# A hybrid decoder layer on one core: the two token halves of the blocked gate/up product become even and odd tiles, and TensorE's order between attention and gate/up is written down

## Chip, core and metric

The kernel runs on one core of a Trainium2 chip. The metric is the device time of one execution in microseconds (us); less is better. Engines are named as in the profile: PE is TensorE, DVE VectorE, ACT ScalarE, POOL GpSimd, SP SyncE, which here only issues DMAs.

## What is computed

One decoder layer on 1024 tokens of width 1024, in f32: an entry LayerNorm, two groups of attention heads, an output projection over the two normalised groups, a LayerNorm, a SwiGLU feed-forward of width 2816, and a last LayerNorm.

```python
h = layer_norm(x, ln_in_g, ln_in_b)
mix = hybrid_mixer(h, ...)                    # merged = [rms_norm(sb_out), rms_norm(swa_out)]; merged @ w_out
h = layer_norm(ALPHA * h + mix, ln1_g, ln1_b) # the stretch that the change rewrites ends here
gate, up = split(h @ w_gate_up)
ffn = (silu(gate) * up) @ w_down
h = layer_norm(ALPHA * h + ffn, ln2_g, ln2_b)
```

## The kernel before

Every f32 matrix product is done as three products of rounded parts (high x high, low x high, high x low), so each operand is first split: ACT casts the high part, and POOL or DVE subtracts it to get the low part. The tokens are eight tiles of 128.

The kernel has three large stretches. Up to about 490 us it projects and attends; the output projection of one head group runs beside the attention and leaves partial sums in `acc_dram`. From about 490 to 580 us comes the stretch of this change. From there to about 1085 us PE multiplies gate and up, and then the down projection follows.

In the stretch of the change `out_load` loads a pair of token tiles of the other head group (`m`), splits it and sums its squares. `out_proj` then goes through the two tiles: a 128x1 product `pr` gives the sum of squares, DVE and POOL make the RMS scale `r` of it, 24 products fill two PSUM tiles `pc` (12 for each half of the width), and DVE (L510) adds `pc` times `r` to the row sums `res`. `ln_apply` normalises `res` in place: DVE statistics (L121, L123, L114, L138), POOL's power for `rstd` (L115), ACT subtracts the mean (L141), DVE scales (L142), POOL adds the bias (L144). The last tile has a form without ACT (L131, L134). `h1_dram` keeps the result for the last LayerNorm.

Gate/up is done as a blocked product with seven instead of eight block products, P1 to P7 (`RIGHT` names their right-hand operands). The tokens are cut into two halves, and the width into `d0` and `d1`. The first half gives `B11` and `B21`, the second `B22`, and the differences of the halves give `T1` to `T4`. `put_b` fills them: four 128x128 transposes on PE into one of the two PSUM banks with the tag "tr", a cast by ACT, a subtraction by DVE. I call this a group. There are 28 of them: 2 for each of four tiles of the first half, 5 for each of the second.

Before the change the halves are tiles 0 to 3 and 4 to 7, so a tile of the second half needs the tile four places before. The pairs run in the order 0, 2, 1, 3 (L620), and each tile's groups are written right after its LayerNorm. The program says nothing of PE's order: Tile's scheduler sets it. Only SP's DMAs can be tied to the order in which they are written, by `Ordered`, and that is off here. All tiles of this stretch come from one pool of 17 buffers of 4 KB (`U`), of which 10 are held by the weights and the LayerNorm's gain and bias.

`prepare` splits the weights of the next blocks, which `left_of` sums by DVE first for P3 and P5 to P7; `gate_up` runs one block of 12 products of 512 columns and adds it up. `seq` is their order.

Of the kernel before, what the change touches and what calls it, by code (L numbers as in the profile page):

```python
# [21 lines left out]
P = 128  # L22
# [52 lines left out]
def layer(ctx: ExitStack, tc: tile.TileContext, x, ln_in, w_sw, w_sb, norm_g,  # L75
          sinks, rel_bias, onehot, w_out, ln1, w_gu, w_down, ln2, out):
    nc = tc.nc
    pe, act, dve, pool = nc.tensor, nc.scalar, nc.vector, nc.gpsimd
    sp = Ordered(tc, nc.sync)
# [142 lines left out]
    def U(shape, name, dt=F32R):  # L222
        return ub.tile(shape, dt, tag="u", name=name)
# [270 lines left out]

    def out_proj(c, m, wo, acc):
        mh, ml, ss = m
        for i in range(2):
# [121 lines left out]

    order = (0, 2, 1, 3)  # L620
    ms = {c: out_load(0, c) for c in order[:2]}
    hs = {}
    d0, d1 = slice(0, 512), slice(512, D)
    for n, c in enumerate(order):
        if n in (1, 2):
            ms[order[n + 1]] = out_load(0, order[n + 1])
        for t, h in out_proj(c, ms[c], wo, load_acc(c, acc_dram)):
            ln_apply(h, h, g1, b1, t == NT - 1)
            sp.dma_start(h1_dram[t], h)
            o = (t % 4) * P  # L630
            if t < 4:
                hs[t] = h
                put_b("B11", h[:, d0], o)
                put_b("B21", h[:, d1], o)
                continue
            h0 = hs.pop(t - 4)
            tt = U([P, 2, 512], "tt", F32)
            pool.tensor_tensor(out=h0[:, d0], in0=h[:, d0], in1=h0[:, d0], op=ALU.subtract)
            pool.tensor_tensor(out=tt[:, 0], in0=h[:, d1], in1=h0[:, d0], op=ALU.subtract)
            dve.tensor_tensor(out=tt[:, 1], in0=h[:, d1], in1=h[:, d0], op=ALU.subtract)  # L640
            pool.tensor_tensor(out=h0[:, d1], in0=h0[:, d1], in1=tt[:, 0], op=ALU.subtract)
            put_b("B22", h[:, d1], o)
            put_b("T2", tt[:, 0], o)
            put_b("T3", tt[:, 1], o)
            put_b("T1", h0[:, d0], o)
            put_b("T4", h0[:, d1], o)


# [3 lines left out]
    fs = [f for i in range(KF) for f in (i, KF + i)]  # L652

    seq = [(fs[0], "P1"), (fs[1], "P1"), (fs[0], "P2"), (fs[1], "P2"), (fs[0], "P6"), (fs[0], "P7")]
    seq += [(fs[0], n) for n in ("P5", "P4", "P3")] + [(fs[1], n) for n in ("P6", "P7", "P5", "P4", "P3")]
    for f in fs[2:]:
# [48 lines left out]

    banks, tmps, acts = {}, {}, {}

    def spill(k, a, b):
# [9 lines left out]
        act.dma_start(a_dram[k][:, 5:7], s[1])  # L718

    def gate_up(i):  # L720
        f, name = seq[i]
# [5 lines left out]
        if name == "P1":  # L727
            tmps[f] = new("t", [P, 2, 512], bufs=2)
            act.copy(tmps[f][:, 0], ps)
            return  # L730
        u2, u3 = tmps[f][:, 0], tmps[f][:, 1]
        if name == "P2":
            acts[f] = new("act", [P, 2, 512], bufs=4)
        a = acts.get(f)
        add = lambda out, x: dve.tensor_tensor(out=out, in0=x, in1=ps, op=ALU.add)  # L735
        if name == "P2":
            act.activation(a[:, 0], ps, AF.Silu)
        elif name == "P6":
            add(u2, u2)
# [15 lines left out]

    prepare(6)
# [4 lines left out]
    for i in range(len(seq)):  # L761
        prepare(i + 6)
        gate_up(i)
# [78 lines left out]
    with tc.tile_pool(name="dn", bufs=4, reuse_waits="tile") as dn:  # L842
        bq += [dn.tile([P, D], F32, tag="bq", bufs=KF + 2, name="bq") for k in range(KF)]
        h = [dn.tile([P, D], F32, tag="h", bufs=NT, name="h") for t in range(NT)]
        LEFT = {"P2": 1, "P4": 2, "P5": 3, "P6": 4, "P7": 5, "P3": 6}
        NEEDS = {"P5": (1,), "P2": (2,), "P3": (3,), "P6": (), "P7": (), "P4": ()}
# [4 lines left out]
        def one(t):  # L851
            ot = dn.tile([P, D], F32, tag="ot", bufs=2, name="ot")
            rows = slice(t * P, (t + 1) * P)
            if t < NT - 1:
# [13 lines left out]
        for name in ("P5", "P2", "P3", "P6", "P7", "P4"):  # L868
# [5 lines left out]
            for k in range(KF):  # L874
# [87 lines left out]
```

## Time and profile before

| | us |
|---|---|
| median of three runs | 1236.27 (1234.16 to 1238.58) |
| the profiled execution | 1236.33 |
| its span | 1234.6 |
| PE busy | 1151.2 (93%) |
| DVE / POOL / ACT busy | 867.5 / 750.0 / 570.9 |

Over the span PE is busy 93% of the time. The page's row of granted clock has its lowest places at the start, near 490 us, and between 530 and 580 us. So the stretch of this change is one of the few in which PE is neither always busy nor always at its full clock. The table gives totals; what the change is worth is read from that stretch alone, by the engines' rows there.

### The profile page before, as it was taken

The numbers are of one execution on the slowest core, as the hardware profiler recorded it, in microseconds if no ns is written. First come the engines' busy times: TensorE is split into PE (matmuls) and PEld (weight loads), VectorE is DVE, ScalarE is ACT, GpSimd is POOL, SyncE is SP. The second block draws the span as 40 slices with busy tenths as digits, with TensorE's granted clock in tenths as the row PEclk, the third lists the DMA queues.
The fourth block names the chain that finished last, engine by engine and source line by source line (L and its number), as shares of the span: only waits on it lengthen the run. The fifth ranks groups of instructions, "written<-read, shape, count | busy, mean of one in ns | idle before, by whom it ended". The sixth has DMA issues, their size and how long they took to land. (4 is left out here: it accounts for less than half of the span.)

```text
span 1234.6 us, 17707 instructions
## 1 busy us (share of the span) xinstructions
PE 1151.2 (93%) x6246; PEld 990.9 (80%) x6246; DVE 867.5 (70%) x1257; ACT 570.9 (46%) x1224; POOL 750.0 (61%) x682
## 2 busy tenths in 40 slices
PE   5698999999998998977999999999999999979997
PEld 4688999899997886765888888888888888757785
DVE  7885786787889894777765645656456349998645
ACT  4565677767678564233433222332232234425531
POOL 5514344556647877567877656666557455774694
PEclk9798999999999898987999999999999999989998
DMA  7213102020105525134333323333323269643441
GB/s 274 93 55 94 35 23 77 23 66 22 49 18 172 186 99 192 73 121 145 119 128 111 103 76 112 111 111 102 95 94 111 95 218 396 212 137 93 114 134 68
DMA packets 60054, 140.69 MB, mean 114 GB/s; under 512 B 7060, under 2 KB 18877, under 8 KB 59966
## 3 DMA queue, kind: packets, MB, share of 16 engines
q1 hardware_dynamic: 45406, 110.71, 28.1%
q10 hardware_dynamic: 14560, 28.85, 6.1%
q8 instruction: 49, 0.80, 0.3%
q14 instruction: 39, 0.32, 0.1%
HBM read 95.75 MB, written 41.17 MB: 111 GB/s over the span
## 5 line engine op out<-in xcount | busy, mean ns | idle before, releaser
L107 POOL TENSOR_TENSOR w<-s,w 128x512 fp32r<-128x512 f32 x88 | 124.1, 1413 | 119.2 <-ACT w L106 119.2
L154 PE MATMUL pp<-xh,whi 128*128 128x256 f32 x544 | 158.8, 293 | 0.0
L154 PE MATMUL pp<-xh,wlo 128*128 128x256 f32 x544 | 158.2, 291 | 0.0
L154 PE MATMUL pp<-xl,whi 128*128 128x256 f32 x544 | 157.5, 290 | 0.0
L776 PE MATMUL pd<-bhl,ahl 128*128 128x512 f32 x612 | 146.6, 400 | 10.0 <-DVE bhl L768 9.6
L776 PEld LDWEIGHTS pd<-bhl,ahl 128*128 128x128 f32 x612 | 117.0, 193 | 39.4 <-DVE bhl L768 14.9
L106 ACT CAST w<-s 128x512 fp32r<-128x512 f32 x88 | 54.4, 622 | 202.7 <-PE pgu L703 118.9
L768 POOL TENSOR_TENSOR ahl<-ar,ahl 128x512 fp32r<-128x512 f32 x63 | 92.6, 1477 | 59.1 <-ACT ahl L767 57.0
L735 DVE TENSOR_TENSOR t<-t,pgu 128x512 f32<-128x512 f32 x88 | 60.1, 683 | 96.6 <-PE pgu L703 96.2
L433 POOL TENSOR_TENSOR s<-s,s 128x127 f32<-128x127 f32 (+2 forms) x96 | 92.6, 969 | 37.7 <-DVE s L429 33.3
L154 PEld LDWEIGHTS pp<-xh,wlo 128*128 128x128 f32 x544 | 106.6, 196 | 1.2
L154 PEld LDWEIGHTS pp<-xl,whi 128*128 128x128 f32 x544 | 106.6, 196 | 1.0
L154 PEld LDWEIGHTS pp<-xh,whi 128*128 128x128 f32 x544 | 106.5, 196 | 0.6
L429 DVE TENSOR_TENSOR_SCAN s<-s,brk 128x128 f32<-128x128 f32 (+1 forms) x64 | 74.7, 1174 | 11.2 <-ACT s L420 10.6
L374 POOL TENSOR_TENSOR L<-L,rd 128x512 f32<-128x512 f32 (+1 forms) x32 | 30.9, 989 | 81.5 <-DVE rd L372 63.9
L110 ACT CAST at<-tra 128x256 fp32r<-128x256 f32 (+1 forms) x160 | 55.5, 356 | 52.7 <-DVE at L111 30.9
L768 DVE TENSOR_TENSOR bhl<-bq,bhl 128x512 fp32r<-128x512 f32 x51 | 67.8, 1338 | 8.2 <-ACT bhl L767 7.9
L111 DVE TENSOR_TENSOR at<-tra,at 128x256 fp32r<-128x256 f32 (+1 forms) x160 | 58.5, 383 | 15.8 <-ACT at L110 14.6
L107 POOL TENSOR_TENSOR w<-gr,w 128x512 fp32r<-128x512 f32 x44 | 61.2, 1405 | 2.3 <-ACT w L106 2.3
L703 PE MATMUL pgu<-B11h,w 128*128 128x512 f32 x176 | 59.1, 398 | 1.4 <-ACT w L106 1.4
L767 ACT CAST ahl<-ar 128x512 fp32r<-128x512 f32 x63 | 38.9, 619 | 43.0 <-POOL ahl L768 17.1
L703 PE MATMUL pgu<-T4h,w 128*128 128x512 f32 x176 | 57.9, 390 | 0.0
(222 smaller groups left out, 3351.2 us busy)
## 6 DMA issues: line engine op xcount, KB each, us to landing
ar<-a_dram SPq DMA_DIRECT2D x73, 256.0 KB, 2.9
a_dram<-act ACTq DMA_DIRECT2D x33, 512.0 KB, 2.6
gr<-in_w_gu SPq DMA_DIRECT2D x24, 512.0 KB, 3.6
ur<-in_w_gu SPq DMA_DIRECT2D x23, 512.0 KB, 3.5
bq<-in_w_down SPq DMA_DIRECT2D x44, 256.0 KB, 4.3
raw<-in_w_sb SPq DMA_DIRECT2D x12, 512.0 KB, 3.4
h_dram<-x ACTq DMA_DIRECT2D x8, 512.0 KB, 3.3
m<-o_dram SPq DMA_DIRECT2D x32, 128.0 KB, 3.0
```

The source lines that it names most:

```text
L106: act.copy(hi, raw)
L107: pool.tensor_tensor(out=lo, in0=raw, in1=_f(hi), op=ALU.subtract)
L110: act.copy(hi, ps)
L111: dve.tensor_tensor(out=lo, in0=ps, in1=_f(hi), op=ALU.subtract)
L154: pe.matmul(ps, a, b, start=(i == 0), stop=(i == n - 1))
L429: dve.tensor_tensor_scan(s2[:, 0:w][:, ::-1], s2[:, 0:w][:, ::-1], brk[:, 512 - w:][:, ::-1] if last else zero.broadcast_to([P, w]), 1.0 i ...
L433: pool.tensor_tensor(out=s1[:, 0:m], in0=s1[:, 0:m], in1=s2[:, 1:m + 1], op=ALU.mult)
L703: pe.matmul(ps, a, b, start=(start and n == 0), stop=(stop and n == 11), skip_group_check=True)
L735: add = lambda out, x: dve.tensor_tensor(out=out, in0=x, in1=ps, op=ALU.add)
L767: act.copy(w[:, 0], src)
L768: eng.tensor_tensor(out=w[:, 1], in0=src, in1=_f(w[:, 0]), op=ALU.subtract)
L776: pe.matmul(pd[t], x, y, start=(first and k == 0 and n == 0), stop=(end and k == KF - 1 and n == 2), skip_group_check=True)
```

## The change

1. The halves become even and odd tiles: `even(t)` fills B11 and B21 from tile t, `odd(t)` forms the differences of tiles t-1 and t and fills B22, T1, T3, T2, T4. Two of the differences are now written in place into the odd tile (except for the last one), which needs no further buffer.
2. The pairs run in the order 0, 1, 2, 3, and the groups of a tile are written two tiles behind: after tile t's products come `even(t-2)`, or B22 of `odd(t-2)`; the four T groups of an odd tile wait one tile more. They stand beside the next even tile's, so there are six groups in a row.
3. PE is wrapped in `Ordered` too, and from the first output projection to the last transposes PE's and SP's instructions keep the order in which they are written. The `pc` products go to the PSUM banks with the tags "z" and "av" instead of "pp".
4. The stores to `h1_dram` are issued by ACT instead of SP.
5. P1 and P2 of the first two features (48 products) are written before the last odd tile's transposes; their P1 results go into one tile `ut`, and their Silu comes later. The weights of nine blocks are prepared from the first load, where before those of the first feature were loaded and summed a second time.
6. The last LayerNorm finds its tiles by `tile_of`, since the halves now hold other tokens.

```diff
-    pe, act, dve, pool = nc.tensor, nc.scalar, nc.vector, nc.gpsimd
+    pe, act, dve, pool = Ordered(tc, nc.tensor), nc.scalar, nc.vector, nc.gpsimd
...
-                ps = bps.tile([P, 512], F32, tag="pp", name="pc")
+                ps = bps.tile([P, 512], F32, tag=banks[d], name="pc")
...
+    seq = [(f, n) for n in ("P1", "P2") for f in fs[:2]]
+    EARLY_GU = len(seq)
+    for f in fs[:2]:
+        seq += [(f, n) for n in ("P6", "P7", "P5", "P4", "P3")]
...
+    def even(t):
+        put_b("B11", hs[t][:, d0], t // 2 * P)
+        put_b("B21", hs[t][:, d1], t // 2 * P)
+
+    def odd(t):
+
+        x, y = hs[t - 1], hs[t]
+        o = t // 2 * P
+        sub(pool, x[:, d0], y[:, d0], x[:, d0])
+        if t < NT - 1:
+            t2, t3 = y[:, d1], y[:, d0]
...
+        sub(dve, t3, y[:, d1], y[:, d0])
+        put_b("B22", y[:, d1], o)
+        if t < NT - 1:
+            sub(pool, t2, y[:, d1], x[:, d0])
+        sub(pool, x[:, d1], x[:, d1], t2)
+        return lambda: [put_b(n, v, o) for n, v in (("T1", x[:, d0]), ("T3", t3), ("T2", t2), ("T4", x[:, d1]))]
...
+    pe.on = sp.on = True
+    for c in range(4):
+        if c in (1, 2):
+            ms.append(out_load(0, c + 1))
+        for t, h in out_proj(c, ms[c], wo, load_acc(c, acc_dram), ("z", "av")):
+            hs[t] = h
+            ln_apply(h, h, g1, b1, t == NT - 1)
+            act.dma_start(h1_dram[t], h)
+            if t >= 2 and t % 2 == 0:
+                even(t - 2)
+                if late:
+                    late.pop()()
+            elif t > 2:
+                late.append(odd(t - 2))
+    even(NT - 2)
+    late.pop()()
+    prepare(5)
+    for i in range(EARLY_GU):
+        gate_up(i)
+    prepare(EARLY_GU + 5)
+    odd(NT - 1)()
+    pe.on = sp.on = False
...
+        tile_of = [2 * (t % 4) + t // 4 for t in range(NT)]
...
-                        sp.dma_start(h[t], h1_dram[t])
+                        sp.dma_start(h[t], h1_dram[tile_of[t]])
```

On every engine the built programs are alike up to the end of the attention and again from about the eighth block of gate/up on; the difference lies between. Three places show it.

PE, behind the products of the first tile that has T groups to follow it. `pc` is a projection's PSUM tile, `pr` the 128x1 product that opens the next tile, `trh` the PSUM tile of a group (x4 is one group), `tt` and `res` what is transposed. Before:

```order
L154 MATMUL pc<-woh,wlo 128x512
L612 MATMUL trh<-ident,tt 128x128 x8
L612 MATMUL trh<-ident,res 128x128 x12
L612 MATMUL trh<-ident,tt 128x128 x8
L501 MATMUL pr<-ones,m 128x1
L154 MATMUL pc<-woh,whi 128x512
```

Now, behind tile 4:

```order
L65 MATMUL pc<-woh,wlo 128x512
L68 MATMUL trh<-ident,res 128x128 x24
L65 MATMUL pr<-ones,m 128x1
L65 MATMUL pc<-woh,whi 128x512
```

Seven groups stood in a row there, of the two tiles that had just been normalised; now it is six, of tiles 1 and 2, and so again behind tile 6 (six) and tile 7 (seven), with single tiles' worth of products between.

SP, at the loads of the third and fourth pair. `m` is an operand of the projection, `res` a tile's row sums, `gr` a gate weight. Before:

```order
L71 DMA res_6437<-acc_dram4_102 128x1024
L71 DMA res_6439<-acc_dram5_103 128x1024
L71 DMA h1_dram0_106<-res_6291 128x1024
L71 DMA h1_dram1_107<-res_6293 128x1024
L71 DMA h1_dram4_110<-res_6437 128x1024
L71 DMA h1_dram5_111<-res_6439 128x1024
L71 DMA m_6627<-o_dram0_90 128x256
```

Now:

```order
L71 DMA res_6411<-acc_dram3_101 128x1024
L71 DMA m_6540<-o_dram0_90 128x256
L71 DMA m_6540<-o_dram1_91 128x256
L71 DMA m_6540<-o_dram2_92 128x256
L71 DMA m_6540<-o_dram3_93 128x256
L71 DMA res_6552<-acc_dram4_102 128x1024
L71 DMA res_6554<-acc_dram5_103 128x1024
L71 DMA res_6713<-acc_dram6_104 128x1024
L71 DMA res_6715<-acc_dram7_105 128x1024
L71 DMA gr_6913<-in_w_gu 128x1024
```

The four stores, which wait for LayerNorms, no longer stand ahead of the loads; all loads up to the first gate weights follow each other.

DVE, behind the last tile's products, in the new program. `res_6715` is that tile's row sums, `s` the sums of weights of the first feature, `B22l`, `B11l` and `B21l` the low parts of groups:

```order
L510 SCALAR_TENSOR_TENSOR res_6715<-pc_6818,r_6816,res_6715 128x512
L652 TENSOR_TENSOR s_6931<-ur_6929 128x512
L654 TENSOR_TENSOR s_6932<-gr_6913,ur_6929 128x512
L121 BN_STATS bst_6846<-res_6715 128x6
L653 TENSOR_TENSOR s_6931<-s_6931,gr_6913 128x512
L510 SCALAR_TENSOR_TENSOR res_6715<-pc_6832,r_6816,res_6715 128x512
L655 TENSOR_TENSOR s_6932<-gr_6913,s_6931 128x512
L617 TENSOR_TENSOR B22l_6257<-trh_6860,B22h_6256 128x4x128
L121 BN_STATS bst_6846<-res_6715 128x6
L617 TENSOR_TENSOR B11l_6253<-trh_6869,B11h_6252 128x4x128
L123 BN_AGGR mv_6849<-bst_6846 128x2
```

The four sums of weights, which stood behind nearly all of the last groups before, now stand between the last tile's residual and the subtractions that free the transposes' banks.

## Rows read from the trace of the kernel before

**Rows 1.** Stretches: from:to, length, busy of PE, PEld, DVE, ACT, POOL; granted clock; DMA.

```profile
490.00:526.00 36.00, 34.14 (x157) 28.06 (x157) 23.27 (x49) 9.72 (x15) 21.49 (x23) 0.94 0.16 62
526.00:542.10 16.10, 8.84 (x38) 6.72 (x37) 9.62 (x18) 6.56 (x11) 11.89 (x10) 0.68 0.59 197
542.10:561.00 18.90, 18.10 (x93) 14.84 (x91) 15.78 (x31) 6.90 (x13) 10.23 (x11) 1.00 0.14 56
561.00:580.00 19.00, 11.09 (x45) 8.61 (x46) 15.28 (x21) 7.31 (x14) 14.84 (x12) 0.64 0.40 139
580.00:660.00 80.00, 80.00 (x355) 65.92 (x354) 51.43 (x57) 30.30 (x53) 59.50 (x42) 1.00 0.35 118
```

**Rows 2.** Timeline of PE: start, duration, instruction, [idle before it, and what ended it].

```profile
490.00 0.42 PE L501 MATMUL pr<-ones,m 128*128 128x1 f32 x2
...
513.21 0.39 PE L154 MATMUL pc<-woh,wlo 128*128 128x512 f32 x1
...
517.29 0.39 PE L154 MATMUL pc<-woh,wlo 128*128 128x512 f32 x1
...
525.79 1.04 PE L612 MATMUL trh<-ident,tt 128*128 128x128 f32 x8
527.85 0.66 PE L612 MATMUL trh<-ident,res 128*128 128x128 f32 x4 [1.02 <-DVE T2l L617]
531.04 1.31 PE L612 MATMUL trh<-ident,res 128*128 128x128 f32 x8 [2.53 <-DVE T3l L617]
533.54 1.94 PE L612 MATMUL trh<-ident,tt 128*128 128x128 f32 x8 [1.20 <-DVE T4l L617]
537.92 0.59 PE L501 MATMUL pr<-ones,m 128*128 128x1 f32 x2 [2.43 <-DVE res L510]
...
541.73 0.61 PE L154 MATMUL pc<-wol,whi 128*128 128x512 f32 x1
542.16 0.42 PE L154 MATMUL pc<-woh,wlo 128*128 128x512 f32 x1
...
561.50 0.66 PE L612 MATMUL trh<-ident,res 128*128 128x128 f32 x4 [0.79 <-POOL res L144]
...
575.69 0.79 PE L703 MATMUL pgu<-B11h,w 128*128 128x512 f32 x1 [1.43 <-ACT w L106]
...
581.36 0.60 PE L612 MATMUL trh<-ident,res 128*128 128x128 f32 x4
```

**Rows 3.** Timeline of SP's DMA queue: start of waiting, time to the last issue.

```profile
505.12 23.75 SPq L71 DMA_DIRECT2D h_dram<-res  x4
529.37 1.81 SPq L71 DMA_DIRECT2D m<-o_dram  x4
```

**Rows 4.** Timeline of DVE in the same stretch.

```profile
509.66 1.41 DVE L142 SCALAR_TENSOR_TENSOR res<-res,rstd,g 128x512 f32<-128x512 f32 x2
...
530.22 0.68 DVE L617 TENSOR_TENSOR T3l<-trh,T3h 128x512 fp32r<-128x512 f32 x1
530.82 0.67 DVE L617 TENSOR_TENSOR T1l<-trh,T1h 128x512 fp32r<-128x512 f32 x1
...
537.12 1.41 DVE L510 SCALAR_TENSOR_TENSOR res<-pc,r,res 128x512 f32<-128x512 f32 x2 [2.96 <-DMA res<-acc_dram]
...
540.29 0.68 DVE L121 BATCH_NORM_STATS2 bst<-res 128x6 f32<-128x512 f32 x1
541.01 0.21 DVE L123 BATCH_NORM_AGGREGATE mv<-bst 128x2 f32<-128x12 f32 x1
...
564.64 2.13 DVE L131 SCALAR_TENSOR_TENSOR res<-res,mv,g 128x1024 f32<-128x1024 f32 x1
```

**Rows 5.** Groups by line, whole span: busy, mean ns of one, idle before.

```profile
L681 DVE TENSOR_TENSOR s<-gr,ur 128x512 f32<-128x512 f32 x23 | 26.6, 1157 | 1.2 <-POOL w L107 1.2
```

**Rows 6.** Timelines of ACT and POOL: a group's cast, and two LayerNorm steps.

```profile
505.51 0.59 ACT L616 CAST B11h<-trh 128x512 fp32r<-128x512 f32 x1 [3.71 <-PE trh L612]
...
522.88 1.34 ACT L141 ACTIVATE res<-res,nmu 128x512 f32<-128x512 f32 x2 [2.05 <-DVE nmu L138]
...
525.59 2.94 POOL L144 TENSOR_TENSOR res<-res,b 128x512 f32<-128x512 f32 x2 [0.87 <-DVE res L142]
```

More of the change, by code (lines that the diff above doesn't have):

```diff
@@ L493, in out_load, with out_proj @@
         return mh, ml, m[:, 0]
-    def out_proj(c, m, wo, acc):
+    def out_proj(c, m, wo, acc, banks=("pp", "pp")):
         mh, ml, ss = m
@@ L618, in put_b @@
                               in1=_f(hi[:, :, o:o + P]), op=ALU.subtract)
[L620 to L646, printed above, removed]
     RIGHT = {"P1": "B11", "P2": "B21", "P3": "B22", "P4": "T4", "P5": "T1", "P6": "T2", "P7": "T3"}
@@ L704, in block @@
                 n += 1
-    banks, tmps, acts = {}, {}, {}
+    banks, tmps, acts, uts = {}, {}, {}, []
     def spill(k, a, b):
@@ L718, in spill, with silu_first @@
         act.dma_start(a_dram[k][:, 5:7], s[1])
+    def silu_first(f):
+        acts[f] = new("act", [P, 2, 512], bufs=4)
+        act.activation(acts[f][:, 0], banks[f, "z"], AF.Silu)
     def gate_up(i):
@@ L727, in gate_up @@
         if name == "P1":
-            tmps[f] = new("t", [P, 2, 512], bufs=2)
-            act.copy(tmps[f][:, 0], ps)
+            if f == fs[0]:
+                uts.append(ws.tile([P, 2, 512], F32, tag="whi", name="ut"))
+            if f in fs[:2]:
+                tmps[f] = [uts[0][:, fs.index(f)]]
+            else:
+                t = new("t", [P, 2, 512], bufs=2)
+                tmps[f] = [t[:, 0], t[:, 1]]
+            act.copy(tmps[f][0], ps)
             return
-        u2, u3 = tmps[f][:, 0], tmps[f][:, 1]
         if name == "P2":
-            acts[f] = new("act", [P, 2, 512], bufs=4)
+            if f not in fs[:2]:
+                silu_first(f)
+            return
+        if len(tmps[f]) == 1 and name == "P7":
+            tmps[f].append(new("t", [P, 2, 512], bufs=2)[:, 1])
+        u2, u3 = tmps[f][0], tmps[f][-1]
         a = acts.get(f)
         add = lambda out, x: dve.tensor_tensor(out=out, in0=x, in1=ps, op=ALU.add)
-        if name == "P2":
-            act.activation(a[:, 0], ps, AF.Silu)
-        elif name == "P6":
+        if name == "P6":
             add(u2, u2)
@@ L754, in gate_up, with sub @@
                 spill(f - KF, acts.pop(f - KF), acts.pop(f))
-    prepare(6)
+    def sub(eng, dst, x, y):
+        eng.tensor_tensor(out=dst, in0=x, in1=y, op=ALU.subtract)
+    def even(t):
[7 more added lines that the diff above has]
+            t2, t3 = y[:, d1], y[:, d0]
+        else:
+            tt = U([P, 2, 512], "tt", F32)
+            t2, t3 = tt[:, 0], tt[:, 1]
+            sub(pool, t2, y[:, d1], x[:, d0])
+        sub(dve, t3, y[:, d1], y[:, d0])
+        put_b("B22", y[:, d1], o)
+        if t < NT - 1:
+            sub(pool, t2, y[:, d1], x[:, d0])
+        sub(pool, x[:, d1], x[:, d1], t2)
+        return lambda: [put_b(n, v, o) for n, v in (("T1", x[:, d0]), ("T3", t3), ("T2", t2), ("T4", x[:, d1]))]
+    d0, d1 = slice(0, 512), slice(512, D)
+    ms = [out_load(0, 0), out_load(0, 1)]
+    hs, late = {}, []
+    pe.on = sp.on = True
[20 more added lines that the diff above has]
+    pe.on = sp.on = False
     raws.clear()
@@ L760, in layer @@
     fw = l_stack.enter_context(tc.tile_pool(name="fw", bufs=1, reuse_waits="tile"))
-    for i in range(len(seq)):
+    for f in fs[:2]:
+        silu_first(f)
+    for i in range(EARLY_GU, len(seq)):
         prepare(i + 6)
@@ L852, in one @@
             ot = dn.tile([P, D], F32, tag="ot", bufs=2, name="ot")
-            rows = slice(t * P, (t + 1) * P)
+            rows = slice(tile_of[t] * P, tile_of[t] * P + P)
             if t < NT - 1:
```

2 lines of the change are left out of this document (removed).

## The prediction, made before the changed kernel was run

> **What bounds the kernel now.** I read the stretches first, then PE's timeline inside the one that the change rewrites, then the queues of the engines that PE waits for there. Behind 580 us PE is busy for 80.00 of 80 us at the full clock [rows 1]; it is the bound, and it stays so through gate/up. The reader is to see that between 490 and 580 us it is not: 1.9 + 7.3 + 0.8 + 7.9 = 17.8 us idle, and in the two stretches that hold most of it the granted clock is 0.68 and 0.64, a part of the time at the lower of its two levels [rows 1]. Both are rows of transposes: seven groups from 525.79 until tile 2 begins at 537.92, and ten from 561.5 until gate products begin at 575.7 [rows 2]. In both PE waits for DVE (T2l, T3l, T4l): a group needs one of two PSUM banks, and DVE's subtraction is what frees a bank. The last wait of the first row, 2.43 us, is for a residual, which itself waited 2.96 us for a load [rows 2, 4]; that load stood on SP behind four stores, which held the queue for 23.75 us [rows 3]. The clock comes back late: from 537.92 to 542.1 the products are 0.43 us apart, and behind that and elsewhere 0.227 (18 steps from 513.21 to 517.29) [rows 2].
>
> So the question is how long the same work takes in the new order. I measure from 490.0, where the projection's first product stands, to where PE has done all projections, all 28 groups and 50 gate products, behind which the programs differ little. Before: 14 gate products lie between 575.69 and the end of the last group at 581.7 [rows 2]; 36 more at 0.227 end at **589.9**.
>
> **The parts of the change.** PE's work is the same in both: no product is added or removed. All that changes is waiting, so I walk through the new order. Prices: a tile's 24 products 5.45; a group's four transposes 0.4, or 0.65 until the last has ended; its cast 0.59; on DVE a group's subtraction 0.60 (rows 0.68 long follow 0.60 apart, and I take this 0.07 off each DVE row), a residual 0.66, a statistic 0.6, the scaling pair 1.33, the three small ones together 0.5, L131 2.06, a difference or sum of weights about 1.1; on ACT the mean's pair 1.34; on POOL the bias pair 2.94 [rows 2, 4, 5, 6].
>
> *Up to the end of tile 4's products.* Only single groups stand between, and their LayerNorms end some microseconds earlier; "z" and "av" give each product its own bank. Four attention products now stand first (0.22 each at the lower level). 490.0 + 0.9 + 27.2 for five tiles + 1.7 for the slow start, which the clock of 0.94 shows [rows 1], + three groups 1.2 + 0.8 for `pr` = 522. Before, the fifth tile was only begun at 537.9 [rows 2]: the change is far ahead here.
>
> *First burst, six groups.* In the order of DVE that goes with it there stand, up to the subtraction that frees the bank of the last group: two residuals, two statistics, the scaling pair of tile 3, B11l, B21l, the small ones, T1l, the scaling pair of tile 4, T3l. 1.3 + 1.2 + 1.3 + 1.2 + 0.5 + 0.6 + 1.3 + 0.6 = 8.0. DVE also waits about 2: T1's cast stands on ACT behind tile 4's mean pair, which needs the small ones (1.34 + 0.59). From 522.3: T3l ends at 532.4, the last group's transposes at 533.1. So 11.1, of which 2.4 are transposes.
>
> *Clock.* PE is then at the lower level: before, a sparse stretch of this length (526 to 538) had that effect [rows 1, 2]. The next 4.1 us run at half speed: 2.0 lost.
>
> *Tile 5, one group, tile 6*: 5.45 + 0.4 + 0.3 + 5.45 = 11.6, and the 2.0: 546.7.
>
> *Second burst, six groups*: residual, statistic, B11l, B21l, small ones, T1l, half a scaling pair, a difference, the other half, T3l: 0.7 + 0.6 + 1.2 + 0.5 + 0.6 + 0.7 + 1.1 + 0.7 + 0.6 = 6.7, some waits of 0.3, and the last transposes: 7.9. 554.6. Tile 7: 5.6, and 2.0 for the clock; no row shows whether it falls here too, I take it that it does: 562.2.
>
> *Third burst, seven groups.* Here the four weight sums stand in front. DVE can start about 2.7 before tile 7's products end, with its first residual: residual 0.7, two sums 2.2, statistic 0.6, sum 1.1, residual 0.7, sum 1.1, B22l 0.6, statistic 0.6, B11l 0.6, small 0.3, L131 2.1, B21l 0.6, T1l 0.6, L134's pair 1.3, T3l 0.6 = 13.7, then the last transposes 0.8: 11.8 behind the products' end. 574.0.
>
> *48 gate products*: 10.9 and 2.0 for the clock: 586.9. They cover the last tile's LayerNorm and differences entirely.
>
> *Last five groups.* Two banks are free at once; the third group waits for B22's cast and subtraction, the last for T3l. At the pace of a bank, 0.65 + 0.59 + 0.68 and 0.1 between = 2.0 for two groups, this takes 4.2, with two of the gate products inside: **591.1**, where the kernel before had 589.9: +1.2.
>
> *Behind it.* The second feature's weights are loaded when the last group is through, and DVE sums them only behind the first feature's P4, 10.5 later; two sums, a cast and a POOL subtraction 1.4 later the block P7 can run, and PE has come to it about 1.3 earlier. In the kernel before nothing waits there (80.00 of 80 us, [rows 1]). +1.3.
>
> *Edits at nothing.* The Silu that comes later and the `ut` tile lie on ACT, busy 30 of 80 us behind 580; two loads and four DVE sums fewer also lie beside a full PE [rows 1]. `tile_of` renames addresses.
>
> *The stores on ACT.* Their issue waits for POOL's bias pair and holds up ACT's next casts. In the walk the pair is through before PE needs the cast; bounds are 0 and, if each of the seven ended last, 7 x 2.9 less the covers, which are large. I take 0. That they leave SP I have counted as load waits that vanish (2.96 on DVE, [rows 4]). The Trainium skill speaks against this: its first page (Trainium Kernel Development and Optimization, Key Constraints) says that queues of several engines share the same 16 DMA engines and that issuing from several saves only the sequencer's issue time. By that the gain would be nothing and the sum some 2.4 higher; the row of 23.75 us differs, since the queue was held there by what its stores waited for, not by the transfers.
>
> **Sum.** 1.2 + 1.3 = +2.5 on the profiled execution's own 1236.33 us (span 1234.6; the median of the runs is 1236.27): about **1239**. The lead at tile 4 (its products end at 522, where they were only begun at 537.9) is paid back in three bursts instead of two, and in the clock falling three times instead of twice.
>
> The bounds of the walk: at the pace of the banks alone six groups take about 5.2 and seven 6.3, which would take 5.9 + 2.7 + 5.5 off the bursts and perhaps 4 of the clock: 1221. At the pace of the kernel before, 12.1 us for seven groups and 14.2 for ten, 1.4 to 1.7 each, six take 8.5 to 10.4 and the last five 7 to 8.6: up to 8 more, with a fourth fall of the clock 10 more: 1249. My walk lies between, nearer to the second.
>
> **Rivals.**
> *DVE is not what paces the bursts (faster).* If the LayerNorm rows that I queue ahead of the subtractions are done earlier, in the tiles before, the bursts run halfway to the banks' pace: 3 + 1.4 + 2.8 off, and one fall of the clock less, 2: 1230. For it: DVE is busy only 23 of 36 us in the first stretch [rows 1], so it has room. Against: DVE's rows run in a fixed queue, and the ones ahead of the subtractions belong to tiles whose products have only just ended.
> *ACT's queue binds (slower).* A store holds ACT until POOL's bias pair is through, and POOL is itself behind in each burst (differences and RMS scales in one queue). It decides from the point at which the pair ends later than the group's transposes; with 2.5 in each burst, and PE then at the lower level in the last burst too (2.0): 1239 + 7.5 = 1246. For it: POOL was the releaser of transposes at 561.50 [rows 2]. Against: in the walk the pair is 2 us early in most places.
> *The order does not hold, or the gate weights land late.* The order is as written on PE and SP. The first gate weight is issued when T2 of tile 3 is transposed, about 551.7; the slowest loads of this stretch took 7.8 from the first issue to their use (529.4 to 537.1, [rows 3, 4]), then come cast and subtraction. PE wants it at 574: some 10 us of cover. If it did bind, some 5 us slower.
>
> **How the numbers follow.** My forecast 0.52, the faster rival 0.22, ACT's queue 0.21, late weights 0.05. A measurement of this kernel tells about 0.3%, 3.7 us, from no change; the forecast's own spread is 1234 to 1244, most of it within that, 0.10 above. So faster 0.23, the same 0.41, slower 0.36. The range reaches to the middles of both rivals and a little beyond: 1227 to 1246.
>
> **What would show it.** Right: tile 4's products end near 522; then sparse rows of transposes of 11, 8 and 12 us with releasers B11l, T1l, T3l on DVE; three stretches at the lower level; gate products from about 574, 48 in a row; the last five groups some 4 us. The walk fails if the bursts end with POOL or ACT as releaser (second rival), if they last 5 to 7 us (first), or if PE stays at the full clock through them. If PE is full from before 585 on, I was wrong about the sign.

## The result, and the profile of the changed kernel

| | before | after |
|---|---|---|
| median (us) | 1235.96 (1234.16 to 1238.58, 4 runs) | 1246.12 (1243.46 to 1248.38, 4 runs) |
| the profiled execution | 1236.33 | 1243.46 |
| its span | 1234.6 | 1241.7 |

The ratio is 1.0089, with a 95% interval of 1.0069 to 1.0109: the changed kernel is slower by 0.9%. A second series of nine runs gave a median of 1242.99 and a ratio of 1.0053 (1.0037 to 1.0069), so the loss is 0.5 to 0.9%; the profiled execution below is 7.1 us longer than the one before. The prediction had +2.5 and a range that ended at 1246.

The same stretches as in [rows 1], with the same columns (from:to, length, busy of PE, PEld, DVE, ACT, POOL, granted clock, DMA):

```profile
490.00:526.00 36.00, 32.61 (x149) 26.84 (x148) 24.73 (x49) 11.25 (x17) 24.83 (x25) 0.93 0.26 92
526.00:542.10 16.10, 11.83 (x44) 9.58 (x45) 9.25 (x18) 3.62 (x7) 8.57 (x7) 0.61 0.50 164
542.10:561.00 18.90, 14.18 (x65) 11.40 (x64) 13.95 (x27) 7.55 (x14) 14.23 (x13) 0.77 0.36 117
561.00:580.00 19.00, 13.28 (x53) 10.44 (x52) 15.78 (x22) 6.43 (x12) 14.88 (x10) 0.69 0.24 79
580.00:660.00 80.00, 76.16 (x339) 61.38 (x339) 43.94 (x50) 28.21 (x50) 51.06 (x36) 1.00 0.29 92
```

Two things differ. The clock is now below 1.00 in every stretch up to 580 us, where the kernel before had 1.00 between 542.1 and 561. And behind 580 us, where PE had been busy for 80.00 of 80 us, it now idles for 3.84; POOL worked 59.50 us there and now works 51.06.

PE's timeline (start, duration, instruction, [idle before it, and what ended it]), the rows that answer [rows 2]: the transposes behind tiles 4, 6 and 7, the last five groups, and two later waits.

```profile
521.57 1.03 PE L68 MATMUL trh<-ident,res 128*128 128x128 f32 x8
527.70 1.97 PE L68 MATMUL trh<-ident,res 128*128 128x128 f32 x8 [5.10 <-DVE B11l L617]
531.32 1.09 PE L68 MATMUL trh<-ident,res 128*128 128x128 f32 x4 [1.65 <-DVE T1l L617]
533.33 1.09 PE L68 MATMUL trh<-ident,res 128*128 128x128 f32 x4 [0.92 <-DVE T3l L617]
534.21 0.43 PE L65 MATMUL pr<-ones,m 128*128 128x1 f32 x2
...
548.05 1.03 PE L68 MATMUL trh<-ident,res 128*128 128x128 f32 x8
...
556.14 1.09 PE L68 MATMUL trh<-ident,res 128*128 128x128 f32 x4 [2.54 <-DVE T3l L617]
557.02 0.43 PE L65 MATMUL pr<-ones,m 128*128 128x1 f32 x2
565.28 1.03 PE L68 MATMUL trh<-ident,res 128*128 128x128 f32 x8
570.25 2.22 PE L68 MATMUL trh<-ident,res 128*128 128x128 f32 x8 [3.93 <-DVE B22l L617]
...
576.21 1.09 PE L68 MATMUL trh<-ident,res 128*128 128x128 f32 x4 [0.64 <-DVE T3l L617]
576.95 0.78 PE L65 MATMUL pgu<-B11h,w 128*128 128x512 f32 x1
...
589.12 1.03 PE L68 MATMUL trh<-ident,res 128*128 128x128 f32 x8
...
608.91 0.74 PE L65 MATMUL pgu<-T3h,w 128*128 128x512 f32 x2 [0.44 <-POOL w L107]
642.52 0.50 PE L65 MATMUL pgu<-T4h,w 128*128 128x512 f32 x1 [2.23 <-DVE t L723]
```

The three bursts are there, and they end with DVE's subtractions as releasers. They last 12.6 us (521.57 to 534.21), 9.0 (548.05 to 557.02) and 11.7 (565.28 to 576.95). The change has a lead behind its fifth tile, tile 4, but it is smaller than the prediction says. In the order of the kernel before, the fifth tile is tile 2, and its products begin here:

```profile
518.66 0.28 PE L501 MATMUL pr<-ones,m 128*128 128x1 f32 x2
```

They end at 525.79 [rows 2]; what begins at 537.92 is the sixth tile, tile 3. So five tiles are done at 521.57 against 525.79, a lead of 4.2 us and not of 16, and PE had transposed five groups by then where it now has three. The bursts take the lead back, and 2.67 us more are lost behind 600 us, in two waits that the kernel before did not have.

DVE's timeline, for [rows 4, 5]: the first burst, the third with the weight sums (L652 to L655), and the rows ahead of the wait at 642 us.

```profile
523.13 1.41 DVE L510 SCALAR_TENSOR_TENSOR res<-pc,r,res 128x512 f32<-128x512 f32 x2 [0.30 <-POOL r L505]
...
530.48 0.69 DVE L617 TENSOR_TENSOR T1l<-trh,T1h 128x512 fp32r<-128x512 f32 x1 [1.87 <-ACT T1h L616]
...
553.64 1.75 DVE L142 SCALAR_TENSOR_TENSOR res<-res,rstd,g 128x512 f32<-128x512 f32 x1
...
563.44 0.79 DVE L652 TENSOR_TENSOR s<-ur 128x512 f32<-128x512 f32 x1
564.16 1.78 DVE L654 TENSOR_TENSOR s<-gr,ur 128x512 f32<-128x512 f32 x1
...
566.46 1.37 DVE L653 TENSOR_TENSOR s<-s,gr 128x512 f32<-128x512 f32 x1
...
568.42 1.09 DVE L655 TENSOR_TENSOR s<-gr,s 128x512 f32<-128x512 f32 x1
569.43 0.68 DVE L617 TENSOR_TENSOR B22l<-trh,B22h 128x512 fp32r<-128x512 f32 x1
...
590.37 0.69 DVE L617 TENSOR_TENSOR B22l<-trh,B22h 128x512 fp32r<-128x512 f32 x1 [11.34 <-ACT B22h L616]
...
638.54 1.66 DVE L652 TENSOR_TENSOR s<-ur 128x512 f32<-128x512 f32 x1 [1.94 <-DMA ur<-in_w_gu]
640.24 1.63 DVE L653 TENSOR_TENSOR s<-s,gr 128x512 f32<-128x512 f32 x1
641.79 1.47 DVE L723 TENSOR_TENSOR t<-t,pgu 128x512 f32<-128x512 f32 x2
```

The sums take 0.79 + 1.78 + 1.37 + 1.09 = 5.0 us ahead of B22l, which PE waits for. Some 10 us later DVE has nothing to do for 11.34 us, while PE runs the 48 early gate products: the sums stand where they cost something. At 638.54 two sums for the next feature wait for a load and then run. Behind them stands P7's add (L723), and P4, which goes on in the same bank, waits for it.

What answers [rows 3] is SP's queue: its four loads of row sums wait for their buffers (24.77 us from 510.48), and no row of PE or DVE in this stretch waits for them. From ACT, for [rows 6], the one cast that a store holds up; the store, issued at 535.42, waits for POOL's bias pair.

```profile
535.79 0.37 ACT L616 CAST T4h<-trh 128x256 fp32r<-128x256 f32 x1 [0.96 <-POOL res L144]
```

### The profile page after: what moved, and what is told of

The parts are those of the page before. It is cut to its first block, busy times and chain, and to the rows that moved or that the text cites. A ratio compares the mean times of both kernels' runs of the same rounds, so it can differ in the third digit from the quotient of the medians.

```text
span 1241.7 us, 17705 instructions
## 1 busy us (share of the span) xinstructions
PE 1155.8 (93%) x6246; PEld 994.8 (80%) x6246; DVE 864.7 (70%) x1253; ACT 570.1 (46%) x1224; POOL 750.4 (60%) x682
## 5 line engine op out<-in xcount | busy, mean ns | idle before, releaser
L723 DVE TENSOR_TENSOR t<-t,pgu 128x512 f32<-128x512 f32 x82 | 56.0, 683 | 91.3 <-PE pgu L65 90.9
L65 PE MATMUL av<-at,v 128*128 128x256 f32 (+2 forms) x380 | 90.2, 318 | 8.7 <-ACT at L110 4.5
L65 PEld LDWEIGHTS av<-at,v 128*128 128x128 f32 x380 | 62.5, 196 | 15.3 <-DVE at L111 6.4
```

What stands on the lines that cost most here:

```text
L65: self._queue(self.eng.matmul(*a, **k))
```

## The experiments

The theory: the bursts cost the time, because two banks are freed by DVE in its queue's order and the clock falls behind each; and late weights of the second feature cost the waits behind 600 us. Rivals: ACT's queue, which the stores hold; or the written order as such. "The burst" is from its first transpose to the next tile's `pr` or the first gate product. A ratio is against the kernel before, with its 95% interval. The changed kernel was run again only beside `four_banks`, `sums_after` and `free_order`, with 1.0053. Since its own ratio was 1.0089 in the first series, a difference of less than some 4 us to the other runs shows nothing by itself; there the rows have to.

### The changed kernel again

> The changed kernel once more, as the base for the others. Its profiled execution took 1243.46 us where the median of its runs was 1246.1. If the difference is only the spread between executions, this run gives a median of 1243 to 1248 and a profile with the same three bursts and the two waits behind 600 us (0.44 for POOL, 2.23 for DVE). If those late waits vary between executions, a slower profile shows them longer.

1242.99 us, ratio 1.0053 (1.0037 to 1.0069). Its profile has the same bursts (the third 11.7 us) and the same waits, 0.45 and 1.94 us. It is the base of what follows, and the difference of 3 us between the two series stays unexplained. The two profiled executions differ by 2.15 us, and 1.71 of that is there before the projection's first product (491.31 against 489.60).

### Four banks for the groups

```diff
-        ps = bps.tile([P, 4, P], F32, tag="tr", name="trh")
+        groups.append(name)
+        ps = bps.tile([P, 4, P], F32, tag=("tr", "pp")[len(groups) % 2], name="trh")
```

> The groups' transposes alternate between the PSUM tags tr and pp, so that four banks serve them instead of two; nothing else is changed. My theory (bursts paced by two banks that DVE frees in its queue's order): PE runs through the first two bursts two groups further before it waits; each burst is shorter by up to the 2 to 5 us that its last two waits hold, and the clock falls less often: 1236 to 1241 against 1246. Rival (the inputs of the groups are late, by POOL's bias pair or ACT's queue): the waits move to the results of LayerNorm and the bursts keep their length: 1245 to 1247. Rival (the late weights of the second feature cost the time): no change either, and the waits behind 600 us stay.

1236.01 us, 0.9988 (0.9972 to 1.0005): the whole loss is gone. PE's timeline of this kernel:

```profile
542.13 1.91 PE L68 MATMUL trh<-ident,res 128*128 128x128 f32 x16
544.77 1.23 PE L68 MATMUL trh<-ident,res 128*128 128x128 f32 x8 [0.73 <-DVE B11l L620]
545.95 0.38 PE L65 MATMUL pr<-ones,m 128*128 128x1 f32 x2
...
555.87 2.82 PE L68 MATMUL trh<-ident,res 128*128 128x128 f32 x12 [2.68 <-POOL res L144]
...
565.11 1.11 PE L68 MATMUL trh<-ident,res 128*128 128x128 f32 x4 [3.99 <-POOL res L749]
```

The second burst falls from 9.0 to 3.8 us and the first from 12.6 to 8.0. The third grows to 14.1: it begins 13.5 us earlier than in the changed kernel (551.76 against 565.28), and now waits for POOL's bias pair (L144) and differences (L749). With banks to spare, POOL is what is late next.

### The weight sums behind the groups

```diff
+            last_sub[:] = [dve.tensor_tensor(out=lw[0][0][:, k0:k0 + n, o:o + P], in0=ps[:, k0:k0 + n],
+                                             in1=_f(hi[:, :, o:o + P]), op=ALU.subtract).ins]
...
+            if fw is None:
+                for i in four:
+                    tc.add_manual_dep(
+                        i.ins, last_sub[0].name,
```

`four` holds the first feature's four sums; each now follows, in DVE's queue, the last subtraction written so far.

> The first feature's four weight sums on DVE are tied behind the last subtraction of the groups that stand before the 48 gate products; the rest is as in the changed kernel. My theory: they stand for 4.3 to 5 us of DVE's time in front of the third burst's subtractions, so the third burst falls from 11.7 to about 7.5 us, the gate products begin near 573 instead of 577 and the time is about 1242. Rival: DVE's own rows of the last LayerNorm (L131, the residuals) end last anyway, and the burst keeps its length within 1 us: 1245 to 1247. A third way: the sums delay the weights of P5 to P3 behind the 48 products, and what the burst gains is lost behind 589 us.

1239.52 us, 1.0021 (1.0008 to 1.0034), 3.5 us less than the changed kernel. Its third burst on PE, 8.4 us instead of 11.7 (the gate products begin at 571.80):

```profile
563.36 1.03 PE L68 MATMUL trh<-ident,res 128*128 128x128 f32 x8
565.77 1.16 PE L68 MATMUL trh<-ident,res 128*128 128x128 f32 x8 [1.38 <-DVE B22l L619]
```

The first wait is 1.38 instead of 3.93 us, and nothing was lost behind the 48 products: the sums had time in DVE's idle 11 us. The later wait is still there: PE idles 2.22 us between 620 and 640.

### TensorE's order left free

```diff
-    pe.on = sp.on = True
+    sp.on = True
```

> TensorE's order in the stretch is left to the scheduler as in the kernel before; SP stays in written order, and the halves, banks, stores and early P1 and P2 stay as changed. If the fixed order itself costs the time, PE's rows spread the groups between the products and the time falls to 1236 to 1240. If the order is the gain of the change and the bursts would else be as before, it rises to 1248 or more. If neither, it stays within 2 us of 1246.

1231.78 us, 0.9960 (0.9941 to 0.9979): 11 us less than the changed kernel, and faster than the kernel before. Stretches of this kernel, columns as above:

```profile
490.00:526.00 36.00, 35.87 (x185) 30.23 (x184) 31.09 (x62) 13.50 (x21) 29.73 (x28) 1.00 0.30 107
526.00:542.10 16.10, 10.11 (x53) 7.88 (x51) 14.92 (x29) 7.48 (x14) 11.95 (x12) 0.85 0.83 296
542.10:561.00 18.90, 7.23 (x28) 5.17 (x28) 18.52 (x21) 5.36 (x11) 18.10 (x13) 0.50 0.20 82
```

PE idles even more in one place, 11.67 us between 542.1 and 561. But DVE, the engine that paces the groups, works 31.09 + 14.92 + 18.52 = 64.5 us up to 561, where the changed kernel's has 24.73 + 9.25 + 13.95 = 47.9. I read this so that it counts how early DVE gets its work, not how much PE waits; the run alone does not show it.

### Second feature's weights early

```diff
-    prepare(EARLY_GU + 5)
+    prepare(EARLY_GU + 10)
```

> The changed kernel, but the weights of the second feature's five other blocks are loaded, summed and split with those of the first, in the written stretch, instead of behind the last transposes. My theory: in the changed kernel they are loaded from 594 us on, DVE and POOL then have more to do than they can between 600 and 660 us, and the waits of 0.44 (POOL) and 2.23 us (DVE) come from that; without them the time falls by 2.7 to 1240, and PE is full from 600 to 680 us. Rival: the waits belong to the first spill of products and the order of the blocks (DVE and POOL rows of that, not weights), then the later wait stays and the time falls by at most 0.5. Against both: DVE's four more weight sums, if they stand before the third burst, make it up to 4.5 us longer.

1247.29 us, 1.0108 (1.0091 to 1.0126). The wait of 0.44 us is gone, but the later one stays:

```profile
572.19 2.21 PE L68 MATMUL trh<-ident,res 128*128 128x128 f32 x8 [7.27 <-DVE B22l L617]
```

```profile
638.43 0.50 PE L65 MATMUL pgu<-T4h,w 128*128 128x512 f32 x1 [1.89 <-DVE t L723]
```

My second theory fell: loading that feature early doesn't remove the later wait. What the text warned of came instead, more sums in front of the third burst, whose first wait is 7.27 us; it lasts 14.9.

### DVE's adds first

```diff
+            if fw is not None and last_add:
+                tc.add_manual_dep(
+                    one.ins, last_add[0].name,
...
-        prepare(i + 6)
+        prepare(i + 5)
```

`one` is the first of a feature's four sums, `last_add` the add of the last P7 before it. The last line also has the weights prepared one block later.

> The changed kernel with the same weights prepared in the same place, but behind the stretch DVE's four sums of the next feature's weights are tied behind the add of P7, which frees the PSUM bank that P4 takes. Loading the second feature's weights early left the later wait (1.89 instead of 2.23 us); so my new account of it is DVE's queue: sums that wait for a load or for POOL stand ahead of that add. If so, the wait near 642 us goes, and the time falls by 1.5 to 2.5: 1241 to 1243.5 where the changed kernel has 1243 to 1246. Rival: the sums then come late for the next feature's blocks and PE waits there instead: no change, or slower by up to 2.

1240.06 us, 1.0034 (1.0018 to 1.0050). PE is busy for 20.00 of 20 us from 620 to 640 and from 640 to 660; the wait at 642 us is gone. By the ratios that is 2.3 us, which alone would show nothing, since the intervals overlap. DVE's timeline shows the add ahead of the sums:

```profile
632.29 0.69 DVE L729 TENSOR_TENSOR t<-t,pgu 128x512 f32<-128x512 f32 x1 [2.03 <-PE pgu L65]
632.90 0.81 DVE L653 TENSOR_TENSOR s<-ur 128x512 f32<-128x512 f32 x1
```

This fits the order in DVE's queue as the cause, and `weights_early` failed because it moved loads and left that order. It isn't the only thing that differs: behind 616 us PE's blocks, whose order is free there, come in another order too.

### Stores on SP, and stores on ACT alone

```diff
-            act.dma_start(h1_dram[t], h)
+            sp.dma_start(h1_dram[t], h)
```

> The changed kernel, but the eight stores to h1_dram are issued by SP, in written order, instead of ACT. My account (the stores on SP hold back the loads behind them until a LayerNorm is done): the row sums of each next pair come late, DVE's residuals wait for loads, and PE waits for the projection's banks at tiles 2, 4 and 6: 5 to 15 us slower than the changed kernel, 1248 to 1258. Rival (ACT's queue is held by the stores, which makes the casts late): 1236 to 1241. If loads are covered anyway and the casts too: 1243 as the changed kernel.

1252.37 us, 1.0157 (1.0135 to 1.0178), in the range that my account had, but not by the loads that I named. SP's queue, then PE:

```profile
501.43 5.18 SPq L71 DMA_DIRECT2D h_dram<-res  x2
506.70 2.16 SPq L71 DMA_DIRECT2D m<-o_dram  x4
```

```profile
519.21 0.58 PE L65 MATMUL pr<-ones,m 128*128 128x1 f32 x2 [6.94 <-POOL m L492]
```

The loads of `m` stand behind two stores that wait for a LayerNorm, and PE waits 6.94 us for what is made of them; I had expected the row sums to be late. The rival, that taking the stores off ACT makes the kernel faster, is out.

The same edit the other way round, alone in the kernel before:

> The kernel before, with the eight stores to h1_dram issued by ACT instead of SP, alone. By my account of the kernel before, the residual's wait of 2.96 us for a load at 537 us goes, and PE's wait of 2.43 us with it, some of it kept by the next thing that is late; the time falls by 1 to 4 us, 1232 to 1235 against 1236. By the skill's rule on issuing queues, which I weighed in the prediction, 1236 as before. Rival (ACT's queue binds): 1237 to 1240.

1234.42 us, 0.9995 (0.9978 to 1.0011): no difference that this measurement can tell. In its trace the wait for the load is gone and tile 3 begins 2.65 us earlier, at 535.27 instead of 537.92 [rows 2]:

```profile
535.27 0.42 PE L501 MATMUL pr<-ones,m 128*128 128x1 f32 x2
```

The last group, at 578.68, is still 2.68 us earlier than in the kernel before (581.36, [rows 2]). Behind the stretch a P4 waits 0.61 us for DVE's add, which it did not before, and the profiled execution is 2.1 us shorter (1234.21 against 1236.33). The interval of the times leaves room both for this and for nothing. The rule that I weighed in the prediction, from the Trainium skill (Trainium Kernel Development and Optimization, Key Constraints), has it that issuing from several engines saves only the sequencer's issue time, so no gain. The time agrees with that rule within its interval, the queue rows don't, and `stores_sp` shows a loss of 1% from moving the stores alone, where SP's order is written down.

### PE kept busy in the bursts

```diff
+        if name != "B22":
+            dm = bps.tile([P, 512], F32, tag="pp", name="dm")
+            for i in range(4):
+                pe.matmul(dm, wo[0][0][:, 0:P], wo[0][0][:, 0:512], start=(i == 0), stop=(i == 3))
```

> The changed kernel with four more products of 512 columns behind each group but those of B22, into a PSUM tile that nothing reads; they add 0.9 us of PE time to each of 24 groups, nearly all of it inside the bursts. It separates the clock from the waits: if PE stays at its upper level through the bursts, the products behind them run at 0.227 us each from the first, which gives back up to 6 us (three falls of 2.0), less what the added products cost where PE would not have waited (some 6 groups in front of each wait, 3 to 8 us). My theory: the granted clock of 526 to 580 us rises from 0.6 to 0.8 to near 1.00, the bursts last as long as before, since DVE paces them, and the time is 1240 to 1246. If the clock falls none the less, it is 1245 to 1252.

1246.67 us, 1.0098 (1.0074 to 1.0123). Stretches of this kernel:

```profile
526.00:542.10 16.10, 13.90 (x70) 11.56 (x70) 10.67 (x20) 2.67 (x5) 8.35 (x8) 1.00 0.39 133
542.10:561.00 18.90, 15.53 (x83) 12.45 (x82) 11.81 (x20) 7.57 (x14) 11.97 (x11) 1.00 0.39 140
```

The clock stays at its upper level through two bursts. Tiles 5 and 6 with their group take 11.8 us instead of 13.8, tile 7 takes 5.7 instead of 8.3: the two falls cost 2.0 and 2.6 us. The 48 gate products behind the third burst take 10.9 instead of 12.2, so that fall cost 1.3. The added products cost as much or more where PE would have gone on (the second burst 10.4 instead of 9.0, the third 15.8 instead of 11.7), and the sum is no gain.

### T groups two and two

```diff
-        return lambda: [put_b(n, v, o) for n, v in (("T1", x[:, d0]), ("T3", t3), ("T2", t2), ("T4", x[:, d1]))]
+        four = (("T1", x[:, d0]), ("T3", t3), ("T2", t2), ("T4", x[:, d1]))
+        return [lambda g=g: [put_b(n, v, o) for n, v in g] for g in (four[:2], four[2:])]
```

> The changed kernel, its written order kept, but an odd tile's four T groups split two and two: T1 and T3 stand behind the next even tile, T2 and T4 behind the next odd one. The rows of transposes are then 4, 3, 4 and 9 groups long instead of 6, 1, 6 and 7. My theory (a written row of groups behind a tile waits for that tile's own LayerNorm rows on DVE): the first two bursts get shorter by the two last groups each, 2 to 4 us each, the last longer by 2 to 3: 1238 to 1243. If only the number of groups counts, no change: 1242 to 1246.

1241.69 us, 1.0048 (1.0031 to 1.0066): not told apart from the changed kernel's second series. Its rows of transposes last 7.4, 2.8, 3.5 and 20.0 us; the row of nine takes back what the others gave, 8.3 us more than the changed kernel's third burst, where I had expected 2 to 3.

### Two edits with the order free, and the banks alone

The free order and the four banks together, by the two diffs shown above:

> Both edits that made the changed kernel faster: TensorE's order in the stretch left to the scheduler, and four banks (the tags tr and pp in turn) for the groups' transposes. If both acted through the same thing (how early DVE is given its work), they do not add: within 3 us of the free order alone, 1229 to 1234 against 1236 of the kernel before. If they act on different waits, they add: 1222 to 1227.

1233.32 us, 0.9988 (0.9969 to 1.0007), no better than the free order alone: the scheduler chose another order, in which PE waits 11.43 us for one LayerNorm.

In the kernel before, the four banks as above, and with them the projection's banks:

```diff
-                ps = bps.tile([P, 512], F32, tag="pp", name="pc")
+                ps = bps.tile([P, 512], F32, tag=("z", "av")[d], name="pc")
```

> The kernel before with nothing but the banks changed: the projections go to the tags z and av, and the groups' transposes to tr and pp in turn. It tells how much of what the free order or four banks reach needs the even and odd halves and the early P1 and P2 at all. If the halves bring nothing: 1229 to 1233, as the free order with the changed halves. If the banks help only when the work is spread over even and odd tiles: 1235 to 1237, as before.

1251.94 us, 1.0118 (1.0095 to 1.0141), which none of the two accounts had. In its trace the projection waits for DVE's residual, 4.59 us at 544.81.

Both show that with a free order an edit to banks also changes the order, so that these two say little on the banks themselves. Whether the even and odd halves bring anything of their own stays open.

### The repairs together

The diffs of the four banks, the sums behind the groups and the adds first, in one kernel:

> The changed kernel with its written order kept and three repairs at once: four banks for the groups, the first feature's weight sums tied behind the groups before the 48 gate products, and the later features' sums tied behind the add of P7. Alone they gave back about 8, 4 and 2 us of the changed kernel's time. If they are separate waits, 1230 to 1233 against 1236 of the kernel before; if four banks already took what the sums cost (in that kernel the third burst waited for POOL, not for sums), 1233 to 1236. If the written order costs time by itself, it stays above the free order with the same repair behind the stretch, by 2 us or more.

1226.36 us, 0.9924 (0.9905 to 0.9943): 0.8% faster than the kernel before, with the change's written order kept, and below the 1230 to 1233 that I had for separate waits. The end of its third burst on PE:

```profile
558.30 1.11 PE L68 MATMUL trh<-ident,res 128*128 128x128 f32 x4 [3.14 <-POOL res L762]
...
560.80 0.77 PE L65 MATMUL pgu<-B11h,w 128*128 128x512 f32 x1
```

The bursts last 8.0, 3.8 and 10.5 us, and the gate products begin at 560.80. Counted from the projection's first product (487.85, and 489.60 in the changed kernel) that is 72.95 instead of 87.35 us. By the ratios, 1.0053 - 0.9924 = 0.0129, or 15.9 us; the three alone gave 8.0, 4.0 and 2.3, which is 14.3. They add up as separate waits would, as far as these intervals tell. What is left of the third burst waits for POOL.

The same, and the T groups two and two:

> The same three repairs, and the T groups split two and two over the next two tiles, which alone was within 2 us of the changed kernel. With four banks the first two bursts no longer wait much, so splitting them should change little: within 2 us of the three repairs. If the last row of nine groups waits for POOL's differences, it is 2 to 4 us slower.

1227.02 us, 0.9927 (0.9907 to 0.9947): the split of the T groups adds nothing.

The free order and the adds first:

> TensorE's order left free, and the sums of the later features' weights tied behind the add of P7, the rest as in the changed kernel. The free order alone took 1231.8 with a wait of 2.15 us for that add. If the two are separate, 1229 to 1230.5, faster than both kernels by 0.4 per cent or more. If the wait only moves to the next feature's blocks, 1231 to 1233.

1228.11 us, 0.9941 (0.9920 to 0.9961). The intervals of this and of `fixed_three` overlap: the best kernel with the written order and the best with the scheduler's are not told apart. They differ in more than the order, three repairs against one, so what the written order costs or gains by itself stays open.

## Why the prediction was wrong, point by point

Two steps failed: the first two bursts were sized too short, by 2.6 us together, and behind the stretch a wait of 2.23 us stood at nothing. The mechanism of the bursts was right.

*What bounds it, and the mechanism*: right. The bursts are DVE's, by their releasers; four banks alone gave 8 us back. *Stores at nothing*: right, by the trace, where a store holds one cast for 0.96 us, no row of PE waits for that, and ACT never ends a burst. (DVE's 1.87 us for T1's cast are the mean pair's, which the walk had as about 2.) That rival's 1246 is the median of the first series, by another mechanism. *DVE not pacing* (1230): out, for the same reason.

*The lead at tile 4*: misread, as said above; 537.9 is the sixth tile's start. The walk did not use it. In the same rows eight groups, not ten, stand between 561.5 and 575.7, so the kernel before took 1.8 us a group there and not 1.4. Against that the first burst, with 2.1, is slow, the other two (1.5 and 1.7) are not.

*The walk*, term by term, measured against predicted: tile 4's end 521.57 (522); first burst 12.6 (11.1); tiles 5 and 6 with the clock's fall 13.8 (13.6); second burst 9.0 (7.9); tile 7 with the fall 8.3 (7.6); third burst 11.7 (11.8); 48 gate products 12.2 (12.9); the last five groups to dense products 4.7 (4.2). The end is 593.8 instead of 591.1: **+3.9** against 589.9, where I had +1.2.

The terms that were mis-sized most are the first two bursts, 2.6 us together, and this is the larger part of the miss. In the first, DVE began the residuals at 523.13 and not at 522.3: it was busy until 522.8 with the rows of the tile before, among them a difference of 1.77 us where I had 1.1, and then waited 0.30 for POOL's scale `r`. The last transposes ran at the clock's lower level, 1.09 us instead of the 0.65 that I took from a row at the upper. In the second, the scaling pair and the difference between T1l and T3l took 2.95 us (552.37 to 555.32) where I had 2.5: one half of the pair alone took 1.75; here, too, the last transposes took 1.09. That the third burst came out right is partly luck: the sums took 4.7 us net where I had 4.4, and L131 1.43 where I had 2.06.

*Behind it, +1.3*: the step that failed in its mechanism. The block P7 waits where I said, but 0.44 us. I put everything else behind the stretch at nothing because nothing waited there before; 2.23 us came 34 us later, from sums that wait for a load ahead of an add in DVE's queue. The kernel before had escaped this narrowly, and its trace says so. From DVE and PE before:

```profile
632.23 1.47 DVE L735 TENSOR_TENSOR t<-t,pgu 128x512 f32<-128x512 f32 x2
```

```profile
632.96 0.50 PE L703 MATMUL pgu<-T4h,w 128*128 128x512 f32 x1
```

The first of the two adds stands behind sums there as well and ends at 632.91; P4 begins at 632.96, 0.34 us behind the product ahead of it, where 0.23 is the pace. So a busy share of 80.00 of 80 us hid a wait that had no room left: with the last group only 2.68 us earlier (`before_stores_act`) a P4 at 631 waits 0.61 us. I had the order of both programs and looked at it only up to the stretch's end. So 2.67 instead of 1.3: together 3.9 + 2.67 = 6.6 of the 7.1 us between the profiled executions; the rest is not placed.

*The clock*: three falls, right; 2.0, 2.6 and 1.3 us by `keep_busy`, against 2.0 each.

*The range*: +7.1 in the profiled execution, 1243.5, lies inside. The median of the first series lies 2.7 above that execution, which is the fastest of its four, and this put the result 0.1 us outside; the second series is inside. Either way the loss is about three to four times the +2.5 that I forecast. The slow rival's terms, 2.5 in each of three bursts and 2.0 for the clock, make 1248.5 and not the 1246 at which I ended the range; a range to its middle would have held the result, for a reason that the runs don't bear out. I gave "within 0.3%" the best chance because 2.5 us lies under that bound. Five of the eight terms of the walk came out longer than I had them, and the two largest errors are in good part of one kind: rows priced from places where they stood alone or at the upper level of the clock.

## What to carry to other kernels

In this kernel, where PE's order is written by hand, the engine that frees its PSUM banks decides: read that engine's queue and ask of every row ahead of a release whether it could stand elsewhere, above all rows whose inputs are not there yet. A row that is idle-time work for its engine (here the sums of weights) costs when it stands ahead of a release: moving the sums' 5.0 us away took 3.3 us off the third burst. And where PE is busy for 100%, walk the queue on to the next few releases behind the change and ask how much room each has: here a release came 0.05 us before PE went on, and any shift could open a wait.

## What the runs showed of the hardware

The same add on DVE, 128x512 from two tiles in SBUF, takes 0.68 or up to 1.78 us. The four sums ahead of the third burst took 5.0 us; tied behind the groups, two of the four took 0.68. The Trainium skill (GPSIMD Engine Reference, Key points) says that POOL shares its SBUF interfaces with DVE and that DVE instructions with two SBUF inputs contend with it. The rows fit. POOL's beside two of the sums above:

```profile
562.39 3.00 POOL L107 TENSOR_TENSOR w<-gr,w 128x512 fp32r<-128x512 f32 x2 [1.64 <-ACT w L106]
566.02 1.26 POOL L746 TENSOR_TENSOR res<-res 128x512 f32<-128x512 f32 x1 [0.63 <-POOL w L107]
```

The sum of 1.78 at 564.16 begins beside the second split and ends 0.55 us behind it (565.94 and 565.39); the one of 1.37 at 566.46 ends 0.55 behind the difference (567.83 and 567.28). So does the slow half of the scaling pair: 555.39, where the half of POOL's bias pair beside it (553.20 to 554.84) ends 0.55 earlier. Free rows follow each other 0.60 us apart, so the extra length is about the time until POOL's row ends; I read it as DVE's row being held until then. DVE's rows with one input in PSUM are not held: B22l at 569.43 takes 0.68 beside a split of POOL. In `sums_after` the sum of 0.68 at 574.62 stands where POOL has no row. That a moved row also changes its own length by a factor of two and a half is what I had averaged away with "about 1.1".
